# 40 instead of 32 expert products made ahead of the dense loop, 8 of them parked in DRAM

## The chip, the core and the metric

The kernel runs on one core of a Trainium2 chip. The metric is the device time in microseconds (us), the median of several executions. The core has five engines that run their own instruction queues in program order: PE (matmul, with its weight loads PEld), DVE (elementwise), ACT (activations and copies), POOL (here: gathers) and SP (here: most DMA issues). ACT and POOL issue DMAs too.

## The reference, cut to what matters

One decoder block for 512 tokens of width 1024: two token mixers (attention and RWKV-7), then a feed-forward part that picks 128 of 16384 experts for each token. The changed lines belong to that last part:

```
s1, s2 = q1 @ sub_keys1.T, q2 @ sub_keys2.T     # 8 heads, 128 keys each side
expert_idx, gates = top 16 of (top 16 of s1 + top 16 of s2), softmax
u   = expert_down[expert_idx]                   # 128 rows of 1024 for each token
act = gelu(einsum('bpd,bphkd->bphk', h, u))
out = einsum('bphk,bphkd->bpd', gates * act, expert_up[expert_idx])
```

## The kernel before, in words

The 512 tokens are four blocks of 128. For blocks 0 and 1 the chosen expert rows are **gathered**: 256 gathers of 1 MB (`peer`, tiles `gl`), each followed by a dot product and an add on DVE (L1118 and L1124). For blocks 2 and 3 (`DENSE`) every expert is computed: the 16384 experts are 128 groups of 128. For group i, `dense_z(i)` multiplies the down rows (`u_raw`, 512 KB) by the 256 tokens and puts gelu of it into a tile of 128x256, a *product*. The **dense loop** in `dense` then runs rounds 0 to 127: it scales product i by the gates (`G`), loads the up rows (`v_raw`, 512 KB), splits both into a high and a low part (`hi_lo`: a CAST on ACT and a subtraction on DVE), and adds three matmuls for each of four accumulators in PSUM (12 matmuls `acc` a round, of the round before).

Products come in two ways. Those with i < `AZ` = 32 are made **ahead** of the loop from unsplit f32 (`ps_z<-hf,u_raw`; a matmul in the code is two MATMUL records here, 16 a product) and stay in four tiles `A` of eight products. The other 96 are made **in the loop** from split operands (`ps_z<-hh,uh`, `hl,uh`, `hh,ul`: 24 matmuls a product), and for these ACT and DVE also split `u_raw`.

The products ahead are steps of a generator. `ZFIRST` = 12 of them are handed out while the last blocks choose their experts (`tail_c` works through eight heads: queries `ps_q`, scores `ps_sc`, top-16 on DVE; then `select` makes `idx`), two after each step, with a later priority. 16 more come between the 16 steps of `dense_spread`, which turns indices and gates into the gate table `gd` in DRAM: each step writes 1 MB from a tile `g_` (three buffers) with a DMA on ACT's queue. The last 4 are drained at the end of the spreading. The loop's first scaling needs the load `G<-gd`, which needs all 16 writes.

The Tile scheduler orders the instructions of each engine by priority and its own estimate of readiness. The gathers are given a late priority and fill in everywhere, also in the dense loop. All of this is one static order for each engine, so an instruction that waits holds everything behind it on its engine.

Of the kernel before, what the change touches and what calls it, by code (L numbers as in the profile page):

```python
# [9 lines left out]
F32 = mybir.dt.float32  # L10
# [9 lines left out]
P = 128  # L20
# [13 lines left out]
PRE = 2  # L34
LATE = 1000
ZLATE = 100
ZFIRST = 12
AZ = 32
NG = 3
BG = [[0.91, 2, 2, 1.0, 2.2, 2.85, 2.45, 1.0], [1.6, 2.28, 1, 0.58, 0.25, 0.5, 0.13, 0.36]]  # L40
ZSTEP = 2
# [105 lines left out]
def build(tc, A, out):  # L147
    nc = tc.nc
    with ExitStack() as ctx:
        _build(ctx, tc, nc, A, out)  # L150


def _build(ctx, tc, nc, A, out):
# [3 lines left out]
    def pool(name, side="left", space=None, stack=ctx):  # L157
        kw = dict(space=space) if space is not None else dict(side=side)
        return stack.enter_context(tc.tile_pool(name=name, bufs=1, **kw))

    cp = pool("cp")
    dp = pool("dp", space=bass.MemoryType.DRAM)
# [10 lines left out]
    def bank(name, tag, bufs):  # L173
        return pp.tile([P, 512], F32, name=name, tag=tag, bufs=bufs)
# [57 lines left out]
    def mm(o, l, r, start=True, stop=True):  # L232
        PE.matmul(o, l, r, start=start, stop=stop)  # L233
# [722 lines left out]
    def tail_c(blocks, M, tops):  # L956
# [23 lines left out]
        for bb, b in enumerate(blocks):  # L980
            nc.scalar.dma_start(x2d[b * P:(b + 1) * P, :], x2[bb])
            hT2 = (hTr if b in DENSE else Mh)("h2T", [P, KT, P])
            h2T.append(hT2)
            rs = norm(x2[bb], flat(hT2))
            V.tensor_scalar(x2[bb], x2[bb], rs, None, op0=ALU.mult)
            for k4 in range(2):
                ps = psum_x("ps_h2T")
                for j in range(4):
                    k = 4 * k4 + j
                    PE.transpose(ps[:, j * P:(j + 1) * P], x2[bb][:, k * P:(k + 1) * P], ident)  # L990
                for j in range(4):
                    k = 4 * k4 + j
                    S.activation(hT2[:, k], ps[:, j * P:(j + 1) * P], AF.Identity, scale=hA2[:, k:k + 1], bias=hB2[:, k:k + 1])
            if b in DENSE:
                dense_h(b, hT2)
                if b == DENSE[-1]:
                    ahead["z"] = dense_ahead()
            yield
# [140 lines left out]
    SUB = 8  # L1139
    GSC = 2.0 ** 14  # L1140
    nd = len(DENSE) * P
    dn, ahead = {}, {}
    gd = dp.tile([P, P // SUB, nd // TB, SUB * TB], F32, name="gd")

    def hi_lo(hi, lo, x):
        S.copy(hi, x)  # L1146
        V.tensor_tensor(lo, x, hi.bitcast(F32), op=ALU.subtract)  # L1147
# [12 lines left out]
    def dense_z(i):  # L1160

        dz = dn["z"]
        hh_, hl_ = dn["h"]
        if i < AZ:
            if i % SUB == 0:
                dn["A"] = dz.tile([P, SUB, nd], F32, name="A", tag="A", bufs=AZ // SUB)
            act = dn["A"][:, i % SUB]
        else:
            act = dn["v"].tile([P, nd], F32, name="act", tag="act", bufs=2)
        u = dz.tile([P, D], F32, name="u_raw", tag="u", bufs=4)  # L1170
        nc.sync.dma_start(u, A["dense"][i, 0])
        if i < AZ:
            zs = ((u, dn["hf"]),)
        else:
            uh = dz.tile([P, D], F32R, name="uh", tag="uh", bufs=2)
            ul = dz.tile([P, D], F32R, name="ul", tag="ul", bufs=2)
            hi_lo(uh, ul, u)
            zs = ((uh, hh_), (uh, hl_), (ul, hh_))
        ps = bank("ps_z", "pr", 3)
        for k in range(KT):  # L1180
            ks = slice(k * P, (k + 1) * P)
            for m, (l, h) in enumerate(zs):
                mm(ps[:, :nd], l[:, ks], h[:, k], k + m == 0, k == KT - 1 and m == len(zs) - 1)
        S.activation(act, ps[:, :nd], AF.Gelu_apprx_tanh)  # L1184
        dn["act"][i] = act

    def dense_ahead():
        for i in range(AZ):
            dense_z(i)
            yield  # L1190

    def dense_spread(sel):
# [4 lines left out]
        with ExitStack() as own:  # L1197
# [12 lines left out]
            for q, (idx, gates) in enumerate(sel):  # L1210
# [8 lines left out]
                for t0 in range(q * P, (q + 1) * P, TB):  # L1219
                    g_ = dn["g"].tile([P, P // SUB, SUB * TB], F32, name="g_", tag="G", bufs=NG)  # L1220
                    gv = g_.rearrange("p j (c t) -> p (j c) t", t=TB)
# [20 lines left out]
    def dense(sel):  # L1242

        n = nd
        for _ in dense_spread(sel):
            step(ahead["z"])
        drain(ahead["z"])
        dn["v"] = de = pool("de", side="right")
        parts = {}

        def gates_of(j):

            if j < P // SUB:
                parts[j] = dn["g"].tile([P, n // TB, SUB, TB], F32, name="G", tag="G", bufs=NG)
                nc.sync.dma_start(parts[j].rearrange("p s c t -> p s (c t)"), gd[:, j])

        gates_of(0)
        gates_of(1)
        acc = [[bank(f"acc{q}{d}", *(("px", 2) if q == 0 else (("pm", 1), ("po", 1))[d])) for d in range(2)]
               for q in range(len(DENSE))]  # L1260
        prev = None
        for i in range(P + 1):
            if i < P:
                if i % SUB == 0:
                    gates_of(i // SUB + 2)
                if i >= AZ:
                    dense_z(i)
                act = dn["act"].pop(i)
                v = dn["w"].tile([P, D], F32, name="v_raw", tag="v", bufs=4)
                nc.sync.dma_start(v, A["dense"][i, 1])  # L1270
                vh = de.tile([P, D], F32R, name="vh", tag="vh", bufs=2)
                vl = de.tile([P, D], F32R, name="vl", tag="vl", bufs=2)
                hi_lo(vh, vl, v)
                a3 = act.rearrange("p (s t) -> p s t", t=TB)
                V.scalar_tensor_tensor(a3, a3, 1.0 / GSC, parts[i // SUB][:, :, i % SUB], op0=ALU.mult, op1=ALU.mult)
                ch = de.tile([P, n], F32R, name="ch", tag="ch", bufs=2)
                cl = de.tile([P, n], F32R, name="cl", tag="cl", bufs=2)
                hi_lo(ch, cl, act)
                cur = (ch, cl, vh, vl)
            if prev is not None:  # L1280
                ch, cl, vh, vl = prev
                for q in range(len(DENSE)):
                    qs = slice(q * P, (q + 1) * P)
                    for d in range(2):
                        ds = slice(d * 512, (d + 1) * 512)
                        for m, (a, b) in enumerate(((ch, vh), (ch, vl), (cl, vh))):
                            mm(acc[q][d], a[:, qs], b[:, ds], i == 1 and m == 0, i == P and m == 2)
            prev = cur
            yield
        gt2 = dn["z"].tile([P, D], F32, name="gt2", tag="u", bufs=4)  # L1290
        nc.sync.dma_start(gt2, mrow[3:4, :].to_broadcast([P, D]))
        for q, b in enumerate(DENSE):
            x2 = dn["w"].tile([P, D], F32, name="x2e", tag="v", bufs=4)
            y = dn["w"].tile([P, D], F32, name="y", tag="v", bufs=4)
            nc.sync.dma_start(x2, x2d[b * P:(b + 1) * P, :])
            for d in range(2):
                ds = slice(d * 512, (d + 1) * 512)
                V.tensor_tensor(y[:, ds], acc[q][d], gt2[:, ds], op=ALU.mult)
                V.tensor_tensor(y[:, ds], y[:, ds], x2[:, ds], op=ALU.add)
            nc.sync.dma_start(out[b * P:(b + 1) * P, :], y)  # L1300
        yield
# [73 lines left out]
    def step(gen, n=1, ahead=0):  # L1375
        for _ in range(n):
            tc.cur_priority -= ahead
            next(gen, None)
            tc.cur_priority += ahead

    def drain(gen):
        for _ in gen:
            pass
# [30 lines left out]
    for _ in streams[1]:  # L1414
        if "z" in ahead and nz < ZFIRST:
            tc.cur_priority += ZLATE
# [11 lines left out]
    for _ in dense([sel[b] for b in DENSE]):  # L1428
        tc.cur_priority += LATE
        step(gather)  # L1430
        tc.cur_priority -= LATE
# [15 lines left out]
```

## Time and profile before

| | |
|---|---|
| time, median of 3 runs (lowest to highest) | 1959.58 us (1954.78 to 1961.55) |
| the profiled execution: its own time, its span | 1955.61 us, 1953.8 us |
| PE busy | 1719.2 us (88%) |
| DVE busy | 1607.6 us (82%) |
| ACT busy | 708.4 us (36%) |
| DMA, mean | 303 GB/s |
| mean granted TensorE clock | 0.944 of full |

Busy time is a share of the whole span, and the stages differ: up to about 1000 us the mixers, to 1180 us the choice of experts for blocks 2 and 3, to 1295 us the spreading of the gates, from 1320 to 1945 us the dense loop. Matmuls are pipelined, so their own durations overlap; what one costs is read from the distance between two starts. The granted clock has two levels, 1.2 and 2.4 GHz, so 0.50 in a stretch is the lower one throughout.

### The profile page before, as it was taken

The page shows a single profiled execution, that of the slowest core. Times are in us where ns is not written, and L with a number is a line of the kernel's source. Part 1 is how long each engine was busy: PE and PEld are TensorE (multiplying, and loading weights), DVE is VectorE, ACT ScalarE, POOL GpSimd, SP SyncE. Part 2 cuts the span into 40 slices and gives each one's busy share as a digit, 9 for nine tenths or more (in the row PEclk, how much of TensorE's full clock was granted, in tenths as well). Part 3 has the DMA queues.
Part 4 walks back from the last instruction along what each step waited for, and adds up shares of the span by engine and source line. Part 5 has one row for each costly group of instructions (what it writes and reads, how often), then busy time and mean ns, then how long its engine had stood idle before and what let it go on. Part 6 is the DMA issues. An engine that isn't in the chain of part 4 may idle for free.

```text
span 1953.8 us, 30403 instructions
## 1 busy us (share of the span) xinstructions
PE 1719.2 (88%) x11066; PEld 1473.3 (75%) x11066; DVE 1607.6 (82%) x3732; ACT 708.4 (36%) x1733; POOL 475.5 (24%) x394
## 2 busy tenths in 40 slices
PE   2789989999899999994769809969999999999998
PEld 2677777778787788883458807857789998888997
DVE  6675446459778898887789999969999999999995
ACT  1243233421323322231131113334555555555553
POOL 1210010000332200233322243421323233343310
PEclk9899999899899999996879959989999999999999
DMA  7744654066986965888989959998999999999993
GB/s 296 260 151 156 233 179 159 23 223 205 359 347 250 352 232 182 325 303 303 372 329 359 338 198 335 371 359 343 400 389 416 415 416 415 416 414 414 415 370 119
DMA packets 151347, 592.95 MB, mean 303 GB/s; under 512 B 13710, under 2 KB 46734, under 8 KB 116380
## 3 DMA queue, kind: packets, MB, share of 16 engines
q1 hardware_dynamic: 76624, 286.17, 39.3%
q0 software_dynamic: 39360, 280.51, 37.0%
q10 hardware_dynamic: 35212, 24.31, 4.0%
q8 instruction: 87, 1.43, 0.3%
q14 instruction: 64, 0.52, 0.1%
HBM read 568.91 MB, written 22.04 MB: 302 GB/s over the span
## 4 chain that ended last, share of the span: by engine, by line
PE 35%; issue 27%; DMA 15%; DVE 12%; POOL 11%; ACT 0%; POOLq 0%; SPq 0%; DVEq 0%; ACTq 0%
POOL gl L1115 11%; DMA gl<-in_experts,ii 6%; PE ps_b L233 4%; PE acc L233 4%; PE ps_z L233 4%; PE ps_gt L233 3%; DMA w_b<-in_w_b 3%; PE ps_q L233 3%; DVE acc L1124 3%; DVE gl L1118 2%; PE ps_m L233 2%; PE ps_mix L233 2%; PE ps_ap L233 2%; PE ps_M L233 2%; PE ps_y L233 1%
## 5 line engine op out<-in xcount | busy, mean ns | idle before, releaser
L1115 POOL DMA_INDIRECT gl<-in_experts,ii x256 | 420.2, 1641 | 959.5 <-DVE acc L1124 690.7
L1118 DVE SCALAR_TENSOR_TENSOR gl<-gl,h2p 128x1024 f32<-128x1024 f32 x256 | 311.4, 1216 | 42.2 <-DMA gl<-in_experts,ii 41.8
L1124 DVE SCALAR_TENSOR_TENSOR acc<-gl,z,acc 128x1024 f32<-128x1024 f32 x256 | 326.7, 1276 | 2.9 <-ACT z L1120 2.2
L233 PE MATMUL ps_z<-hh,ul 128*128 128x256 f32 x768 | 217.7, 283 | 3.3 <-DVE ul L1147 3.3
L233 PE MATMUL ps_z<-hh,uh 128*128 128x256 f32 x768 | 217.5, 283 | 0.4 <-ACT act L1184 0.4
L233 PE MATMUL ps_z<-hl,uh 128*128 128x256 f32 x768 | 217.6, 283 | 0.0
L233 PE MATMUL acc<-vh,ch 128*128 128x512 f32 x512 | 197.0, 394 | 16.7 <-ACT ch L1146 16.4
L233 PE MATMUL acc<-vh,cl 128*128 128x512 f32 x512 | 202.9, 396 | 3.1 <-DVE cl L1147 3.1
L233 PE MATMUL acc<-vl,ch 128*128 128x512 f32 x512 | 202.5, 396 | 0.7 <-DVE vl L1147 0.7
L1119 ACT ACTIVATE z<-z 128x1 f32<-128x1 f32 x256 | 52.1, 204 | 373.9 <-DVE gl L1118 373.5
L1147 DVE TENSOR_TENSOR vl<-v_raw,vh 128x1024 fp32r<-128x1024 f32 x128 | 156.2, 1220 | 6.8 <-ACT vh L1146 6.6
L233 PEld LDWEIGHTS ps_z<-hh,uh 128*128 128x128 f32 x768 | 146.8, 191 | 4.1 <-ACT act L1184 0.6
L233 PEld LDWEIGHTS ps_z<-hl,uh 128*128 128x128 f32 x768 | 147.1, 192 | 3.6 <-issue 0.2
L233 PEld LDWEIGHTS ps_z<-hh,ul 128*128 128x128 f32 x768 | 147.0, 191 | 3.8 <-DVE ul L1147 3.7
L233 PE MATMUL ps_z<-hf,u_raw 128*128 128x256 f32 x512 | 132.2, 392 | 15.0 <-ACT i1T L1215 15.0
L233 PE MATMUL ps_gt<-hT,w_b 128*128 128x128 f32 x1024 | 136.3, 287 | 9.8 <-DMA w_b<-in_w_b 7.7
L233 PE MATMUL ps_b<-hT,w_b 128*128 128x128 f32 x896 | 127.0, 293 | 14.1 <-DMA w_b<-in_w_b 12.2
L233 PEld LDWEIGHTS ps_gt<-hT,w_b 128*128 128x128 f32 x1024 | 127.2, 200 | 15.7 <-issue 9.6
L1146 ACT CAST vh<-v_raw 128x1024 fp32r<-128x1024 f32 x128 | 134.0, 1048 | 13.2 <-DMA v_raw<-in_dense 8.5
L233 PEld LDWEIGHTS ps_b<-hT,w_b 128*128 128x128 f32 x896 | 116.3, 205 | 24.8 <-issue 10.6
L233 PE MATMUL ps_q<-h2T,w_q 128*128 128x128 f32 x1024 | 127.7, 278 | 1.9 <-DMA w_q<-in_w_query 1.8
L233 PEld LDWEIGHTS ps_q<-h2T,w_q 128*128 128x128 f32 x1024 | 124.3, 194 | 5.1 <-DMA w_q<-in_w_query 2.2
(430 smaller groups left out, 3306.7 us busy)
## 6 DMA issues: line engine op xcount, KB each, us to landing
u_raw<-in_dense SPq DMA_DIRECT2D x128, 512.0 KB
v_raw<-in_dense SPq DMA_DIRECT2D x128, 512.0 KB
w_b<-in_w_b SPq DMA_DIRECT2D x90, 512.0 KB
w_q<-in_w_query SPq DMA_DIRECT2D x48, 512.0 KB
w_ada<-in_w_ada SPq DMA_DIRECT2D x32, 512.0 KB
G<-gd SPq DMA_DIRECT2D x16, 1024.0 KB
w_o<-in_w_o SPq DMA_DIRECT2D x24, 512.0 KB
w_out<-in_w_out SPq DMA_DIRECT2D x24, 512.0 KB
```

The lines of the kernel that those rows point to most:

```text
L233: PE.matmul(o, l, r, start=start, stop=stop)
L1115: G.indirect_dma_start(out=gl, out_offset=None, in_=A["experts"], in_offset=bass.IndirectOffsetOnAxis(ap=ii[:, s:s + 1], axis=0))
L1118: V.scalar_tensor_tensor(gl[:, :D], gl[:, :D], 1.0, h2, op0=ALU.mult, op1=ALU.mult, accum_out=z[:, 0:1])
L1119: S.activation(z[:, 1:2], z[:, 0:1], AF.Gelu_apprx_tanh)
L1124: V.scalar_tensor_tensor(acc, gl[:, D:], z[:, 1:2], acc, op0=ALU.mult, op1=ALU.add)
L1146: S.copy(hi, x)
L1147: V.tensor_tensor(lo, x, hi.bitcast(F32), op=ALU.subtract)
```

## The change

40 products are made ahead instead of 32. `ZFIRST` is 20 instead of 12, so the eight more are handed out before the spreading; 16 still come between its steps and 4 at its end, so these are now products 20 to 39. The four tiles `A` still hold only 32. Products 32 to 39 go through a tile `zp` with two buffers and are written to a DRAM tensor `zd` (128 KB each) by a DMA on ACT's queue. At round 24 a new tile `A` (the buffer of rounds 0 to 7) is loaded with all eight (1 MB, SP's queue). The loop makes 88 products instead of 96.

```diff
-ZFIRST = 12
+ZFIRST = 20
 AZ = 32
+PZ = 8
...
+    zd = dp.tile([P, PZ, nd], F32, name="zd")
...
             act = dn["A"][:, i % SUB]
+        elif i < AZ + PZ:
+            act = dz.tile([P, nd], F32, name="zp", tag="zp", bufs=2)
         else:
...
-        if i < AZ:
+        if i < AZ + PZ:
             zs = ((u, dn["hf"]),)
...
         S.activation(act, ps[:, :nd], AF.Gelu_apprx_tanh)
-        dn["act"][i] = act
+        if AZ <= i < AZ + PZ:
+            nc.scalar.dma_start(zd[:, i - AZ], act)
+        else:
+            dn["act"][i] = act
 
     def dense_ahead():
-        for i in range(AZ):
+        for i in range(AZ + PZ):
...
                     gates_of(i // SUB + 2)
-                if i >= AZ:
+                    if AZ <= i + SUB < AZ + PZ:
+                        t = dn["z"].tile([P, SUB, nd], F32, name="A", tag="A", bufs=AZ // SUB)
+                        nc.sync.dma_start(t, zd[:, i + SUB - AZ:i + 2 * SUB - AZ])
+                        for j in range(SUB):
+                            dn["act"][i + SUB + j] = t[:, j]
+                if i >= AZ + PZ:
                     dense_z(i)
```

What it does to the order is seen in three places. The first is PE, between the queries of the last head (`ps_q`), its scores (`ps_sc`) and the transposes `ps_igT` that open the spreading. Before:

```order
L233 MATMUL ps_q<-h2T,w_q 128x128 x28
L233 MATMUL ps_sc<-sk,qTp 128x128 x4
L1214 MATMUL ps_igT<-cst,idx_8611 128x128 x2
L1214 MATMUL ps_igT<-cst,gates_8582 128x128
L233 MATMUL ps_z<-hf,u_raw 128x256 x6
```

And of the change:

```order
L234 MATMUL ps_q<-h2T,w_q 128x128 x29
L234 MATMUL ps_z<-hf,u_raw 128x256 x2
L234 MATMUL ps_sc<-sk,qTp 128x128 x4
L234 MATMUL ps_z<-hf,u_raw 128x256 x46
L1221 MATMUL ps_igT<-cst,idx_8709 128x128 x2
L1221 MATMUL ps_igT<-cst,gates_8656 128x128
L234 MATMUL ps_z<-hf,u_raw 128x256 x6
```

46 matmuls of products (eight a product in this listing, so nearly six products) now stand behind the last scores; the other two products more stand between the scores of the last two heads. In the spreading itself the pattern of `ps_z` and `ps_G` on PE is nearly that of before.

The second place is ACT, in the spreading steps 10 and 11 of 16 (`ps_G` is copied into `g_`, which is then written to `gd`; `A` or `zp` receives gelu of a product; `z` belongs to the gathers). Before:

```order
L1238 COPY g__9324<-ps_G 128x128x4 x2
L1119 ACTIVATE z<-z 128x1
L1239 DMA gd<-g__9324 2048x1x128
L1238 COPY g__9392<-ps_G 128x128x4 x2
L1184 ACTIVATE A<-ps_z 128x256
L1120 ACTIVATE z<-z,gates_6211 128x1
L1238 COPY g__9392<-ps_G 128x128x4 x2
L1119 ACTIVATE z<-z 128x1
L1239 DMA gd<-g__9392 2048x1x128
```

And of the change:

```order
L1188 ACTIVATE zp<-ps_z 128x256
L1190 DMA zd<-zp 128x256
L1245 COPY g__9422<-ps_G 128x128x4 x2
L1246 DMA gd<-g__9422 2048x1x128
L1245 COPY g__9490<-ps_G 128x128x4 x2
L1188 ACTIVATE zp<-ps_z 128x256
L1120 ACTIVATE z<-z 128x1
L1190 DMA zd<-zp 128x256
L1121 ACTIVATE z<-z,gates_6212 128x1
L1245 COPY g__9490<-ps_G 128x128x4 x2
L1246 DMA gd<-g__9490 2048x1x128
```

The eight `zd` writes alternate with the `gd` writes of steps 10 to 15 on the one queue, and each `zp` from the third on stands ahead of copies of `ps_G`.

The third place is the end of the dense loop on DVE: the last 12 rows ahead of the closing `y<-acc` (`vl` is the low part of `v_raw`, one a round; `ul` that of `u_raw`, one for each product made in the loop; L1132 of the change closes the gathers). Before:

```order
L1275 SCALAR_TENSOR_TENSOR act<-act,G 128x256
L1147 TENSOR_TENSOR cl<-act,ch 128x256
L1147 TENSOR_TENSOR vl<-v_raw,vh 128x1024
L1147 TENSOR_TENSOR ul<-u_raw,uh 128x1024
L1275 SCALAR_TENSOR_TENSOR act<-act,G 128x256
L1147 TENSOR_TENSOR cl<-act,ch 128x256
L1147 TENSOR_TENSOR vl<-v_raw,vh 128x1024
L1275 SCALAR_TENSOR_TENSOR act<-act,G 128x256
L1147 TENSOR_TENSOR cl<-act,ch 128x256
L1147 TENSOR_TENSOR vl<-v_raw,vh 128x1024
L1275 SCALAR_TENSOR_TENSOR act<-act,G 128x256
L1147 TENSOR_TENSOR cl<-act,ch 128x256
```

And of the change:

```order
L1132 TENSOR_TENSOR acc<-acc,e 128x1024
L1149 TENSOR_TENSOR cl<-act,ch 128x256
L1149 TENSOR_TENSOR vl<-v_raw,vh 128x1024
L1149 TENSOR_TENSOR ul<-u_raw,uh 128x1024
L1287 SCALAR_TENSOR_TENSOR act<-act,G 128x256
L1149 TENSOR_TENSOR cl<-act,ch 128x256
L1149 TENSOR_TENSOR vl<-v_raw,vh 128x1024
L1287 SCALAR_TENSOR_TENSOR act<-act,G 128x256
L1149 TENSOR_TENSOR cl<-act,ch 128x256
L1149 TENSOR_TENSOR vl<-v_raw,vh 128x1024
L1287 SCALAR_TENSOR_TENSOR act<-act,G 128x256
L1149 TENSOR_TENSOR cl<-act,ch 128x256
```

The gathers close five rounds nearer to the end: behind the add of the last gather stand nine `vl` and seven `ul` before, and four `vl` and two `ul` in the change. Up to there each round of either version holds about as many gathers. The loads of the spreading and of the loop on SP's queue are in the order of before, with `A<-zd` among the `v_raw` loads of the first rounds; POOL's order is the same.

## Rows read from the trace of the kernel before

**Rows 1.** Windows, one stretch: busy us (instructions) by engine, clock, DMA share

```profile
core 0: us, PE busy (x) PEld busy (x) DVE busy (x) ACT busy (x) POOL busy (x), PEclk, DMA share, GB/s
1123.00:1157.00 34.00, 0.97 (x9) 0.79 (x8) 34.00 (x120) 3.58 (x10) 13.90 (x5) 0.53 0.53 195
```

**Rows 2.** Windows of the dense loop, columns as in rows 1 (PE to POOL)

```profile
1320.00:1420.00 100.00, 98.61 (x413) 78.36 (x414) 95.98 (x147) 54.63 (x101) 23.39 (x13) 0.97 0.95 371
...
1520.00:1620.00 100.00, 100.00 (x644) 91.01 (x643) 99.20 (x132) 55.38 (x112) 35.40 (x20) 1.00 1.02 415
...
1900.00:1954.00 54.00, 46.97 (x294) 42.18 (x293) 30.38 (x42) 20.14 (x31) 0.00 (x0) 0.97 0.39 133
```

**Rows 3.** End of the chain: start us, us, engine and tile

```profile
1933.01 2.87 PE ps_z L233 x24
1938.63 2.87 PE ps_z L233 x24
1941.50 3.44 PE acc L233 x15
```

**Rows 4.** Waits of PE in the dense loop: us in total, times, longest

```profile
PE acc L233 <- ACT ch L1146: 16.4, 2, 16.3
PE acc L233 <- DVE cl L1147: 3.1, 9, 1.0
```

**Rows 5.** Timeline of DVE around the last gather: start us, us, line, operation

```profile
1890.34 1.21 DVE L1118 SCALAR_TENSOR_TENSOR gl<-gl,h2p 128x1024 f32<-128x1024 f32 x1
...
1891.48 1.22 DVE L1147 TENSOR_TENSOR vl<-v_raw,vh 128x1024 fp32r<-128x1024 f32 x1
1892.62 1.27 DVE L1124 SCALAR_TENSOR_TENSOR acc<-gl,z,acc 128x1024 f32<-128x1024 f32 x1
1893.82 0.41 DVE L1275 SCALAR_TENSOR_TENSOR act<-act,G 128x256 f32<-128x256 f32 x1
1894.15 1.21 DVE L1147 TENSOR_TENSOR ul<-u_raw,uh 128x1024 fp32r<-128x1024 f32 x1
...
1895.63 1.27 DVE L1124 SCALAR_TENSOR_TENSOR acc<-gl,z,acc 128x1024 f32<-128x1024 f32 x1
```

**Rows 6.** Timeline of PE, choice of experts; in brackets idle time and releaser

```profile
1063.93 4.91 PE L233 MATMUL ps_z<-hf,u_raw 128*128 128x256 f32 x22
...
1156.92 0.48 PE L1214 MATMUL ps_igT<-cst,idx 128*128 128x128 f32 x1 [33.02 <-DVE idx L1089]
...
1174.54 5.22 PE L233 MATMUL ps_z<-hf,u_raw 128*128 128x256 f32 x12 [15.02 <-ACT i1T L1215]
```

**Rows 7.** Timeline of ACT in the spreading (ACTq: a DMA issue)

```profile
1239.55 0.52 ACTq L1239 DMA_DIRECT2D gd<-g__9256  x1
...
1244.85 0.39 ACT L1184 ACTIVATE A<-ps_z 128x256 f32<-128x256 f32 x1 [1.67 <-PE ps_z L233]
...
1256.12 1.07 ACT L1238 COPY g__9460<-ps_G 128x512 f32<-128x512 f32 x2 [2.59 <-DMA gd<-g__9256]
...
1267.77 5.22 ACTq L1239 DMA_DIRECT2D gd<-g__9528  x1
...
1281.48 0.39 ACT L1184 ACTIVATE A<-ps_z 128x256 f32<-128x256 f32 x1 [1.07 <-PE ps_z L233]
...
1288.21 1.07 ACT L1238 COPY g__9733<-ps_G 128x512 f32<-128x512 f32 x2 [4.95 <-DMA gd<-g__9528]
...
1292.59 0.52 ACTq L1239 DMA_DIRECT2D gd<-g__9733  x1
```

**Rows 8.** Timeline of all engines at the start of the dense loop

```profile
1315.12 1.28 SPq L1255 DMA_DIRECT2D G<-gd  x3
...
1319.81 1.10 DVE L1275 SCALAR_TENSOR_TENSOR A<-A,G 128x256 f32<-128x256 f32 x3 [13.68 <-DMA G<-gd]
...
1320.73 0.80 PE L233 MATMUL acc<-vh,ch 128*128 128x512 f32 x1 [16.26 <-ACT ch L1146]
```

**Rows 9.** DMA queue of ACT, 1160 to 1330 us: packets, MB, share of 16 engines

```profile
q10 hardware_dynamic: 33024, 16.78, 33.0%
```

## Prediction, made before the change was run

> **What bounds the kernel now.** The profile's own execution took 1955.6 us, 4.0 under the median of the runs shown (1959.6); the sum is made against its own time. First I read the chain of what ended last, from its end. There a round of the dense loop starts every 5.62 us (1933.01 to 1938.63), 2.87 us of it the 24 matmuls of a product, so 2.75 us the twelve of `acc`, and the last matmul starts to drain at 1944.9 [rows 3]. Then the windows of the loop: PE, DVE and the DMA are all full at once (100.00 and 99.20 us of 100, 415 GB/s), and only after the last gather, from 1900 us on, is there room: DVE 30.38 us of 54, DMA 133 GB/s [rows 2]. Which of the three is the bound is told by who waits: apart from one wait of 16.3 us at the start, PE lost 3.1 us to DVE in the whole loop [rows 4]. PE's own work sets its length, with DVE close behind.
>
> Next the two places where PE has nothing to do. One lies between the last scores and the spreading: 33.0 us, then 15.0 us more [rows 6], while DVE is busy for all of a window of 34 us that lies in it, the granted clock is 0.53 and the DMA is half used (0.53, 195 GB/s) [rows 1]. The other is the start of the loop: PE starts at 1320.7 after 16.3 us of idling, ACT waited for DVE's first scaling, and that waited for `G<-gd` [rows 8], issued at 1315.1, when the last `gd` write, issued at 1292.6, had landed [rows 7, 8].
>
> **The change part by part.**
>
> *Taken from the loop:* eight products of 2.87 us on PE [rows 3], 23.0 us. DVE loses eight `ul` of 1.14 us (1890.34 to 1891.48 is the distance of such a row to the next [rows 5]), 9.1 us, and the DMA 4.2 MB of `u_raw`.
>
> *Added ahead:* eight products of 16 records. 22 of them took 4.91 us, so about 0.22 us each at the upper clock and 3.5 us a product; after the idle time 12 took 5.22 us, 0.43 us each, 6.9 us a product at the lower clock [rows 6]. Six stand behind the last scores: 21 us, 41 at the lower clock, in 33.0 us of idle time, and the 15.0 us behind it are idle for another reason, so neither delays the transposes that matter. The eight 512 KB loads fall where the DMA is half used; the later ones share SP's queue with `h2p` of the next gather block, and at most wait for a product each. Their gelus, with the exponentials of `select` now between them, need few of ACT's 30 idle us there [rows 1]. If that cover were gone, all eight would cost 28 us. The other two stand ahead of the last scores, which so come up to 7 us later. DVE, which is never idle there, has gathers in its order to do first. Bounds 0 and 7 us; I take 1, since the order gives DVE the same number of gathers before the spreading.
>
> *The writes:* eight of 128 KB on ACT's queue, among sixteen of 1 MB. Those already fall behind: the ninth landed by 1256.1, the thirteenth by 1288.2, the last by 1315.1 (the copy or load that waited for each [rows 7, 8]), four writes in 32.1 us and three in 26.9, 8.0 and 9.0 us for each. ACT's issue itself took 5.22 us once [rows 7]. The loop starts when this queue is empty, so bytes added to it count. Eight writes are the bytes of one `gd` write, at most 9 us; by packets they are 1024 beside 33024 [rows 9], half of a `gd` write, 4 us; if the other queues give way, nothing. I take 5, near the count of packets.
>
> *The wait of `zp`:* two buffers, so from the third product on the gelu waits for the landing of the write two before, and behind it on ACT stand the copies of `ps_G` and the `gd` writes. As long as a `gd` write is on its way during such a wait, the queue that sets the loop's start stays busy, and the wait costs nothing beyond the bytes above. I take 0 and make the upper end a rival.
>
> *The load `A<-zd`:* 1 MB, needed at round 32, 88 us after the loop's start at 2.75 us a round; its buffer is free after round 8. With the `u_raw` loads gone the loop moves 3.1 MB less. 0.
>
> *DVE in the shorter loop:* a gather costs 2.34 us on DVE (1890.34 to 1891.48 and 1892.62 to 1893.82), a round 2.96 (`act` 0.33, `ul` and `cl` 1.48 to the next add, `vl` 1.14 [rows 5]; the same again within 0.01). Up to the last gather DVE now has five more rounds to do, +14.8, eight `ul` less, −9.1, and by the order one gather more after the loop's start, +2.3: the last add, 575.8 us after the start (1319.8 to 1895.6 [rows 5, 8]), comes at 583.8. From there the loop took 49.3 us, 20.1 of it seven products, so 29.2 us or 10.6 rounds for nine `vl`. With four `vl` and two products it takes 5.6 rounds of 2.75 and 5.7 us, 21.1. Together 604.9 against 625.1: 20.2 us less, where PE alone would give 23.0. So DVE keeps 3 of it.
>
> Sum: 1955.6 − 23.0 + 3 (DVE) + 5 (writes) + 1 (scores) = 1941.6. The runs scatter by 7 us and the profiled one is in their lower half; I add half of its 4.0 and say **1943.5**. A difference under 0.3%, about 6 us, can't be told from no change here.
>
> **The rivals.**
>
> *The writes are hidden as well* and DVE finds its time: 1955.6 − 23.0 + 2 = 1934.6. For it: the small writes are one seventeenth of the queue's bytes. Against it: the queue was behind when the last was issued, 22.5 us before it landed [rows 7, 8].
>
> *DVE and the gathers are the bound*, and PE's saving turns into waits: then the loop shrinks by what DVE loses, 9.1 us, less 6 for the later start: 1955.6 − 3 + 2 = 1954.6, too little to be told from no change; half of it would still show (1948). For it: 99.20 us of 100, and 415 GB/s [rows 2]. Against it: the free time after 1900 us, which is where the gathers can spread to.
>
> *Two buffers are too few* (the other side). If a small write takes as long to land as a `gd` write, 16.6 us (1239.55 to 1256.12), 20.4 or 22.5 us [rows 7, 8], the eighth gelu comes three landings after the second: 67.5 us at the longest, where the last eight gelus of before took 36.6 us (1244.85 to 1281.48 [rows 7]). ACT, and with it the copies and `gd` writes, would then be 31 us late: 1955.6 − 20 + 31 + 1 = 1967.6, slower by 0.6%. It decides from a landing of 18.5 us on (3 × 18.5 − 36.6 = 19). Against it: those times include the wait behind two or three earlier 1 MB writes, and an ACT that is held issues none; behind one write it is 8 to 9 us and the rest of a second. The Trainium skill, page "DMA: Bandwidth & Descriptors", section "Queues, rings and completion order", speaks for this rival: each DMA engine takes a queue's descriptors in ring order, so a small write queues behind the `gd` write before it. The trace agrees so far that `gd` writes land one after the other, 8 to 9 us apart [rows 7, 8]. The same page, section "Anatomy of one DMA — SWDGE (gpsimd) path", fits one DMA alone at 2.0 us plus its bytes over 436 GB/s; by that a 128 KB write lands in an estimated 2.3 us, no gelu waits, and the sum would lose its 5 us: 1936.6 on the profile's scale. The 1 MB writes of this case took four to five times what that fit gives them, so I go by the rows.
>
> **How the numbers follow.** Forecast 0.60 (1936 to 1950: the writes from 0 to 9 us, the scores from 0 to 7, DVE from 0 to 5, 2 us of scatter); writes hidden 0.12; DVE and gathers the bound 0.12, half of it showing as faster; two buffers too few 0.16, of which 0.06 only eat the gain and 0.10 make it slower. Faster by over 0.3%: 0.60 + 0.12 + 0.06 = 0.78; within 0.3%: 0.06 + 0.06 = 0.12; slower: 0.10. The range 1931 to 1958 leaves out the slow end of the last rival and a little below the second.
>
> **What would show it.** In the changed profile: the 33 us gap on PE filled by `ps_z<-hf,u_raw`, with the clock at its upper level there; the spreading's first `ps_G` where it was, within some us; ACT's waits for `zd<-zp` few and short; `G<-gd` issued 3 to 9 us later than 1315.1; rounds of 5.62 us at the end of the loop, the last gather's add within some 25 us of the last matmul; and from the loop's start to the last matmul 602 to 606 us. The prediction is wrong if ACT waits for `zd` by tens of us, or if PE waits for `vl` and `cl` by more than some 5 us in the loop.

## The result, and the profile after

The change took 1935.34 us (median of 9 runs, 1924.71 to 1946.50) beside 1958.20 for the kernel before (9 runs): a ratio of 0.991, 95% interval 0.9883 to 0.9938, that is 12 to 23 us faster. The forecast was 1943.5. The profiled execution took 1931.73 us, its span 1930.0.

Before anything else the two traces have to be brought to one starting point. All five engines run the same instructions in the same order up to the queries of the last block, and yet the first transpose of `ps_h2T`, ahead of them, stands 13.3 us earlier in the changed kernel. Timeline of PE, before and after (the idle time ahead of the row in brackets):

```profile
996.40 1.97 PE L990 MATMUL ps_h2T<-cst,x 128*128 128x128 f32 x8 [10.87 <-DVE rsg L272]
```

```profile
983.09 1.97 PE L991 MATMUL ps_h2T<-cst,x 128*128 128x128 f32 x8 [10.88 <-DVE rsg L273]
```

In the profiles of this study that row starts anywhere from 983.1 to 999.9 us, whatever the kernel. So 13.3 of the 23.8 us between the two spans are scatter of the mixers, and the profiles can be compared only from this row on. I cut them there into three stretches by rows of PE: the **choice** of experts (first `ps_h2T` to first `ps_igT` of the spreading), the **spreading** (to the first `acc`), the **loop** (to the end of the last `acc` row; 2.0 us more than the chain's reading in the prediction, in both kernels).

| kernel | choice | spreading | loop | sum | ratio to before (interval) |
|---|---|---|---|---|---|
| before | 160.5 | 163.8 | 626.2 | 950.6 | 1 |
| the change | 166.6 | 163.4 | 610.1 | 940.0 | 0.991 (0.9883 to 0.9938) |
| e1_place | 164.7 | 163.7 | 625.0 | 953.4 | 0.9961 (0.9931 to 0.9991) |
| e2_number | 162.3 | 174.0 | 624.4 | 960.7 | 1.0026 (0.9991 to 1.0061) |
| e3_actout | 163.1 | 170.9 | 610.0 | 944.0 | 0.9941 (0.9914 to 0.9968) |
| e4_sp | 167.1 | 162.1 | 607.2 | 936.3 | 0.9874 (0.9835 to 0.9912) |
| e5_again | | | | | 0.9882 (0.9857 to 0.9907) |
| e6_zp4 | 164.7 | 163.7 | 610.1 | 938.5 | 0.9909 (0.9877 to 0.994) |
| e7_keep5 | 166.6 | 158.9 | 612.1 | 937.6 | 0.9903 (0.9874 to 0.9933) |
| e8_pz16 | 184.8 | 157.6 | 591.5 | 933.8 | 0.9926 (0.9902 to 0.995) |
| e9_park5 | 166.0 | 166.1 | 609.6 | 941.7 | 0.9948 (0.9916 to 0.998) |
| e10_keep5 | 166.7 | 157.1 | 611.4 | 935.2 | 0.9889 (0.984 to 0.9938) |
| e11_sp | 168.1 | 166.2 | 606.0 | 940.3 | 0.9912 (0.988 to 0.9944) |
| e12_keep5_z24 | 167.3 | 158.0 | 608.5 | 933.8 | 0.992 (0.9889 to 0.9952) |

Each stretch is that of one execution. The profile of e5_again fell into a disturbed execution (1958.59 us; its other runs took 1929.36 to 1937.59), so its stretches are left out.

**The choice.** Timeline of PE: the last scores before, and the rows after that answer to [rows 6]:

```profile
1122.73 1.16 PE L233 MATMUL ps_sc<-sk,qTp 128*128 128x128 f32 x8 [2.17 <-ACT qTp L1025]
```

```profile
1116.94 1.13 PE L234 MATMUL ps_sc<-sk,qTp 128*128 128x128 f32 x8
1117.91 20.02 PE L234 MATMUL ps_z<-hf,u_raw 128*128 128x256 f32 x92
1149.69 0.45 PE L1221 MATMUL ps_igT<-cst,idx 128*128 128x128 f32 x1 [11.76 <-DVE idx L1090]
...
1164.82 4.55 PE L234 MATMUL ps_z<-hf,u_raw 128*128 128x256 f32 x12 [12.61 <-ACT i1T L1222]
```

The six products stand in the gap that was empty, 0.22 us a matmul, and 11.76 us of it are left. The windows show the granted clock at its upper level over these products (1.00), where the gap of before had shown 0.53, and the DMA at 325 GB/s (columns as in [rows 1]; from 1150 us on, behind the transposes, the mean is 0.63, so the lower level for much of that stretch):

```profile
1118.00:1138.00 20.00, 19.93 (x93) 17.20 (x91) 20.00 (x83) 6.09 (x14) 4.50 (x4) 1.00 0.89 325
1150.00:1175.00 25.00, 10.86 (x64) 8.63 (x64) 25.00 (x57) 5.70 (x15) 6.74 (x3) 0.63 0.53 186
```

**The spreading.** Timeline of ACT, after, answering to [rows 7]. Small writes now hold ACT in their issue, and the next gelu stands behind it:

```profile
1257.08 8.41 ACTq L1190 DMA_DIRECT2D zd<-zp  x1
...
1265.59 0.38 ACT L1188 ACTIVATE zp<-ps_z 128x256 f32<-128x256 f32 x1 [7.84 <-issue]
...
1277.40 7.25 ACTq L1190 DMA_DIRECT2D zd<-zp  x1
...
1292.62 0.52 ACTq L1246 DMA_DIRECT2D gd<-g__9836  x1
```

The last `gd` write stands at 1292.6 in both traces, but that is not the same place: counted from the first transpose it is issued after 142.9 us (1292.62 − 1149.69), before after 135.7 (1292.59 − 1156.92, [rows 6, 7]). So ACT is 7.3 us later with it.

**The start of the loop.** Timelines of SP, DVE and PE, after, answering to [rows 8]: from the first `ps_h2T` to the issue of `G<-gd` it is 324.0 us (1307.09 − 983.09), 5.3 more than before (1315.12 − 996.40 = 318.7). Those 5.3 lie in the choice: from the first transpose it is 157.4 us, before 158.2. The last `gd` write, issued 7.3 us later, was followed by `G<-gd` after 14.5 us where before it took 22.5.

```profile
1307.09 1.76 SPq L1262 DMA_DIRECT2D G<-gd  x3
...
1312.15 1.09 DVE L1287 SCALAR_TENSOR_TENSOR A<-A,G 128x256 f32<-128x256 f32 x3 [5.14 <-DMA G<-gd]
...
1313.07 0.80 PE L234 MATMUL acc<-vh,ch 128*128 128x512 f32 x1 [9.50 <-ACT ch L1148]
```

**The loop.** PE's waits in it, after (us in total, times, longest), answering to [rows 4]:

```profile
PE acc L234 <- ACT ch L1148: 9.8, 2, 9.5
PE acc L234 <- DVE vl L1149: 4.3, 3, 3.7
PE acc L234 <- DVE cl L1149: 2.4, 7, 0.8
PE acc L234 <- ACT vh L1148: 1.4, 1, 1.4
```

The wait of 3.7 us for `vl` is new. Timelines of SP and DVE show where it comes from: the reload is issued at 1343.52, DVE reaches the first scaling of a reloaded product at 1351.8, in round 14 and not in 32, and stands there for 3.99 us; the `vl` that PE needs is queued behind it.

```profile
1343.52 0.50 SPq L1275 DMA_DIRECT2D A<-zd  x1
...
1351.42 0.42 DVE L1149 TENSOR_TENSOR cl<-A,ch 128x256 fp32r<-128x256 f32 x1
1355.83 0.42 DVE L1287 SCALAR_TENSOR_TENSOR A<-A,G 128x256 f32<-128x256 f32 x1 [3.99 <-DMA A<-zd]
...
1357.18 1.22 DVE L1149 TENSOR_TENSOR vl<-v_raw,vh 128x1024 fp32r<-128x1024 f32 x1
```

At the end a round still takes 5.62 us (the chain, answering to [rows 3]), and the add of the last gather (timeline of DVE, as in [rows 5]) now stands 21 us ahead of the chain's end instead of 49:

```profile
1909.17 2.87 PE ps_z L234 x24
1912.04 2.75 PE acc L234 x12
1914.79 2.87 PE ps_z L234 x24
1917.66 3.45 PE acc L234 x15
```

```profile
1900.06 1.27 DVE L1125 SCALAR_TENSOR_TENSOR acc<-gl,z,acc 128x1024 f32<-128x1024 f32 x1
```

### The profile page after: what moved, and what is told of

The parts are those of the page before. It is cut to its first block, busy times and chain, and to the rows that moved or that the text cites. A ratio compares the mean times of both kernels' runs of the same rounds, so it can differ in the third digit from the quotient of the medians.

```text
span 1930.0 us, 30268 instructions
## 1 busy us (share of the span) xinstructions
PE 1712.6 (89%) x11002; PEld 1465.1 (76%) x11002; DVE 1597.4 (83%) x3724; ACT 702.8 (36%) x1727; POOL 447.9 (23%) x394
## 4 chain that ended last, share of the span: by engine, by line
issue 31%; PE 28%; DMA 14%; POOL 13%; DVE 12%; ACT 1%; POOLq 0%; SPq 0%; DVEq 0%; ACTq 0%
POOL gl L1116 13%; DMA gl<-in_experts,ii 6%; PE ps_b L234 4%; PE ps_q L234 3%; DMA w_b<-in_w_b 3%; PE ps_gt L234 3%; DVE acc L1125 2%; DVE gl L1119 2%; DMA w_out<-in_w_out 2%; PE ps_m L234 2%; PE ps_ap L234 2%; PE ps_mix L234 2%; DMA w_ada<-in_w_ada 2%; PE ps_y L234 1%; PE ps_s L234 1%
## 5 line engine op out<-in xcount | busy, mean ns | idle before, releaser
L1116 POOL DMA_INDIRECT gl<-in_experts,ii x256 | 393.6, 1537 | 988.5 <-DVE acc L1125 727.1
L234 PE MATMUL ps_z<-hh,ul 128*128 128x256 f32 x704 | 199.5, 283 | 2.4 <-DVE ul L1149 2.4
L234 PE MATMUL ps_z<-hh,uh 128*128 128x256 f32 x704 | 199.4, 283 | 0.4 <-ACT act L1188 0.4
L234 PE MATMUL ps_z<-hl,uh 128*128 128x256 f32 x704 | 199.6, 283 | 0.0
L234 PE MATMUL ps_z<-hf,u_raw 128*128 128x256 f32 x640 | 160.2, 391 | 12.6 <-ACT i1T L1222 12.6
L234 PEld LDWEIGHTS ps_z<-hf,u_raw 128*128 128x128 f32 x640 | 116.9, 195 | 31.6 <-ACT i1T L1222 13.0
L1148 ACT CAST vh<-v_raw 128x1024 fp32r<-128x1024 f32 x128 | 134.1, 1048 | 16.2 <-DMA v_raw<-in_dense 10.1
L234 PEld LDWEIGHTS ps_z<-hh,uh 128*128 128x128 f32 x704 | 134.6, 191 | 7.0 <-issue 3.1
L234 PEld LDWEIGHTS ps_gt<-hT,w_b 128*128 128x128 f32 x1024 | 126.0, 199 | 16.2 <-issue 11.1
L234 PEld LDWEIGHTS ps_z<-hl,uh 128*128 128x128 f32 x704 | 134.8, 192 | 3.1
L234 PEld LDWEIGHTS ps_z<-hh,ul 128*128 128x128 f32 x704 | 134.7, 191 | 2.7 <-DVE ul L1149 2.6
```

The lines of the kernel that those rows point to most:

```text
L1116: G.indirect_dma_start(out=gl, out_offset=None, in_=A["experts"], in_offset=bass.IndirectOffsetOnAxis(ap=ii[:, s:s + 1], axis=0))
```

## The experiments

My theory after the result: the gain is the loop's shorter PE work, 23.0 us, less small prices ahead of it (the later scores, the writes) and less the stand at the reload. The main rival: the gain comes from filling PE's empty time ahead of the spreading. Twelve runs were made: nine other kernels, two of them twice, and the change once more.

**e1_place and e2_number: the two halves of the change alone.**

```diff
-PZ = 8            # e1: 20 ahead of the spreading, 32 in all
+PZ = 0
...
-ZFIRST = 20       # e2: 40 in all, 12 ahead of the spreading
+ZFIRST = 12
```

> Placement alone: 20 products ahead of the spreading as in the change, but 32 products in all, none in DRAM, 96 made in the loop. Three stretches are compared, by rows of PE: choice (first ps_h2T to first ps_igT: 160.5 us before, 166.6 in the change), spreading (to the first acc: 163.8 and 163.4), loop (to the end of the last acc: 624.2 and 608.0). Theory (the gain is the loop's shorter work, less small costs ahead of it): choice 164 to 168, spreading 150 to 164, loop 622 to 626; time within 10 us of before. Rival (the gain comes from filling PE's empty time ahead of the spreading, so the clock is higher behind it): choice and spreading together 10 us or more shorter than before, and the time at least 10 us below before.

> Number alone: 40 products, eight of them through DRAM as in the change, but only 12 ahead of the spreading, so 28 come in it and at its end. Theory: choice as before (160 to 161 us), loop as in the change (606 to 610), spreading longer than before by what of eight products (28 us at the upper clock) the wait for the last gd write does not cover, 5 to 22 us; time from 12 us below before to 8 above. Rival (placement is the gain): no gain left, and 15 us or more slower than the change.

e1: choice 164.7, spreading 163.7, loop 625.0; ratio 0.9961, 1950.38 us beside 1953.57. Choice and spreading together are 4.1 us longer than before, where the rival had them 10 us shorter, and the loop is that of before. In time the interval leaves a gain of 2 to 13 us, so a part of the change's gain in time is not excluded here; its trace from the first `ps_h2T` on, 2.8 us longer than before, shows none.

e2: spreading 174.0, 10.2 longer than before, as the theory has it; but the loop took 624.4 and not 606 to 610. The reason is in the order: before and in the change, five products of the loop stand ahead of its first `acc` on PE (4.7 in the change), where PE waits for `G` anyway; in e2 none does, because the products at the end of the spreading have taken that place, so its loop contains 4.7 more than the change's, 13.5 us by 2.87 each (610.1 and 13.5 are 623.6). The gain is gone (ratio 1.0026). Both halves are needed: eight products fewer in the loop pay only if the eight have an empty place ahead of it.

**e3_actout: the reloaded products scaled into another tile.**

```diff
+                if AZ <= i < AZ + PZ:
+                    act = de.tile([P, n], F32, name="act", tag="act", bufs=2)
+                s3 = act.rearrange("p (s t) -> p s t", t=TB)
-                V.scalar_tensor_tensor(a3, a3, ...)
+                V.scalar_tensor_tensor(s3, a3, ...)
```

> The change, with the scaling of the eight reloaded products into a tile of two buffers instead of in place, so that DVE reaches it some rounds later. Theory: in the change DVE stood 4.0 us at the first such scaling, waiting for the reload, and PE 3.8 us for the low part queued behind it; here that wait is 0 to 1 us and the loop 603 to 606 us instead of 608.0, other stretches unchanged. Rival (the loop there is held by the loads of v_raw, which come late anyway): the wait goes to v_raw and the loop stays at 607 to 609.

Nothing waits for `zd` any more, and DVE's 4.0 us are gone. But the loop took 610.0 us. Two things took the gain. The loads of `v_raw` come late in that part as well (the waits of its first 150 us):

```profile
ACT vh L1148 <- DMA v_raw<-in_dense: 12.4, 8, 3.7
...
PE acc L234 <- ACT vh L1148: 2.3, 1, 2.3
PE acc L234 <- DVE vl L1149: 1.3, 3, 0.5
PE acc L234 <- DVE cl L1149: 0.4, 1, 0.4
```

which is 4.0 us of PE's waits beside 5.7 for `vl` and `vh` in the change. And the scaled products hold the two `act` buffers, so by the order only three products of the loop stand ahead of its first `acc` instead of 4.7: 4.9 us more inside it (41 matmuls of 0.12). So theory and rival were each half right on the wait, and this kernel's time says nothing on it. Its spreading took 170.9 us, 7.5 more than the change's, with that part in the change's order or nearly so: one execution can differ by that much.

**e4_sp and e11_sp: the eight writes on SP's queue.**

```diff
-            nc.scalar.dma_start(zd[:, i - AZ], act)
+            nc.sync.dma_start(zd[:, i - AZ], act)
```

> The change, with the eight writes of parked products issued by SP instead of ACT. In the change four of these issues held ACT for 4.15, 4.14, 8.41 and 7.25 us, and yet the last gd write was issued at the same distance from the transposes as before. Theory: those stalls only take the place of waits that the gd writes would have had, and spreading gets shorter by 0 to 3 us (161 to 164). Rival (ACT's stalls are the price of the writes): spreading shorter by 10 us or more. A second rival (the two buffers): a write on SP's queue lands later, ACT waits for zp, and spreading gets longer by 5 us or more.

> e4_sp once more with more rounds: by the theory that the writes cost the gd queue their bytes and ACT its stalls, time 2 to 6 us below the change (ratio to before 0.986 to 0.990); if moving them changes nothing, 0.990 to 0.993.

Spreading took 162.1 and 166.2 us, with the writes on ACT 163.4 (the change) and 163.7 (e6). On SP an issue takes 0.33 to 1.24 us. In e11 (the rows that touch `zd`: ns min/median/max):

```profile
L1190 SPq DMA_DIRECT2D zd<-zp x8: 326/422/1242, 1246.9 to 1290.1; - x8
L1275 SPq DMA_DIRECT2D A<-zd x1: 424/424/424, 1351.8 to 1351.8; - x1
```

ACT is held all the same, now in its 1 MB issues. Its timeline in e4:

```profile
1257.95 6.34 ACTq L1246 DMA_DIRECT2D gd<-g__9490  x1
...
1289.76 5.19 ACTq L1246 DMA_DIRECT2D gd<-g__9766  x1
```

The issues of `gd` and `zd` that held ACT for over 1 us add up to 30.4 us in e4 and 17.3 in e11, to 29.3 in the change (24.0 of them in small writes) and 19.9 before. So the stalls pass to the `gd` writes, as the theory has it (its "same distance" for the last `gd` write is a misreading: 142.9 us and 135.7, see above). The spreading does not follow them: in e11 ACT was held 12 us less than in the change, and the spreading is 2.8 longer. Both rivals of e4 are out by their own bounds, but a spreading without such stalls was not tried. The times, 0.9874 and 0.9912, lie on both sides of the change, and cannot be told from it.

In both runs nobody waited for the reload, and the loops, 607.2 and 606.0, are 3 to 4 us shorter than the change's. DVE came for it no later: 8.4 us after its issue, in the change 8.3. So the load landed sooner. The DMA queues in these 8.3 us, in the change and below it in e11 (packets, MB, share of 16 engines; q0 carries the gathers, q1 SP's loads):

```profile
q0 software_dynamic: 234, 1.65, 50.7%
q1 hardware_dynamic: 364, 1.67, 49.8%
```

```profile
q1 hardware_dynamic: 371, 1.89, 59.9%
q0 software_dynamic: 138, 1.05, 30.3%
```

The late landing goes with more of the gathers beside the load. e4 (1.05 MB) and e6 (1.61 MB, with the wait) fit this; no run changed the gathers alone.

**e5_again and e6_zp4: the change once more, and with four `zp` buffers.**

```diff
-            act = dz.tile([P, nd], F32, name="zp", tag="zp", bufs=2)
+            act = dz.tile([P, nd], F32, name="zp", tag="zp", bufs=4)
```

> The change once more, as it is: how much of its stretches is its own and how much one execution. Theory: choice 163 to 168 us, spreading 161 to 171, loop 607 to 611; the wait of DVE for the reload anywhere from 0 to 4 us, since e4_sp with the same place of the scaling did not show it. Rival (the 4.0 us wait for the reload is fixed by the order): it comes again, 3 to 5 us.

> The change with four zp buffers instead of two. Theory: what held ACT in the change were the issues of the writes on its own queue, not a zp buffer that a landing had to free; spreading stays at 161 to 171 us, and ACT's issues of zd writes still take 4 to 8 us three or four times. Rival (two buffers are too few): spreading 5 us or more shorter than e5_again of this call, and the stalls gone.

e5 repeats the change's time (ratio 0.9882). In e6 no `zp` waits for a landing any more, and still the issues stall ACT and the spreading takes 163.7 us. Rows of `zp` in e6, and below them what ended ACT's idle time ahead of them:

```profile
L1190 ACTq DMA_DIRECT2D zd<-zp x8: 327/2626/7076, 1242.9 to 1291.1; - x8
...
  issue: 6.5, 1
```

So in the change the two buffers were not what held ACT. The reload was waited for again: DVE 3.9 us, PE 3.5 us for `vl`, with the loop at 610.1 as in the change.

**e7_keep5, e9_park5, e10_keep5: the trip through DRAM by itself.** e7 and e10 are one kernel: 37 products ahead, the five beyond the tiles `A` in five `zp` tiles that are used where they lie. e9 sends the same five through DRAM.

```diff
-PZ = 8
+PZ = 5
...
-            act = dz.tile([P, nd], F32, name="zp", tag="zp", bufs=2)     # e7, e10
+            act = dz.tile([P, nd], F32, name="zp", tag="zp", bufs=PZ)
...
-                        nc.sync.dma_start(t, zd[:, ...])                  # e9
+                        nc.sync.dma_start(t[:, :PZ], zd)
```

> 37 products ahead, five beyond the four tiles kept in SBUF, nothing written to DRAM and nothing reloaded; 91 products in the loop. Theory (the DRAM trip costs 0 to 3 us, a product in the loop 2.87): loop 612 to 616 us, spreading 158 to 170 as in the change, time 4 to 9 us above the change. Rival (the trip through DRAM eats a good part of the gain): as fast as the change or faster, though three more products are made in the loop.

> 37 products ahead as in e7_keep5, but the five beyond the tiles go through DRAM as in the change (two zp buffers, five writes, one reload of 640 KB). Against e10_keep5 of this call it has the trip and nothing else. Theory after the runs so far (the trip costs about 4 us in the spreading and about 4 at the reload, eight in all for eight products): spreading 3 to 6 us longer than e10_keep5, loop 2 to 5 longer, time 3 to 9 us longer. Rival (the trip is free, and e7_keep5's shorter spreading was one execution): both stretches within 2 us, time within 3.

> e7_keep5 once more, beside e9_park5: spreading 156 to 163 us, loop 610 to 614, time 15 to 21 us below before by the theory that the trip is not free; if it was one execution, spreading 161 to 170 and time 10 to 14 below before.

e7 (0.9903) cannot be told from the change (0.991), though three more products, 8.6 us, stand in its loop. Its loop and its spreading lie in the theory's bounds, and its ratio lies between those of the change (e5) and of e6 measured beside it, 0.9882 and 0.9909. So neither theory nor rival is settled by it, and e9 was made to size the trip. Timeline of PE, the first transpose and the first `acc`, in e9 (with the trip) and in e10 (without):

```profile
1160.81 0.45 PE L1221 MATMUL ps_igT<-cst,idx 128*128 128x128 f32 x1 [13.22 <-DVE idx L1090]
...
1326.89 0.79 PE L234 MATMUL acc<-vh,ch 128*128 128x512 f32 x1 [12.36 <-ACT ch L1148]
```

```profile
1166.46 0.45 PE L1217 MATMUL ps_igT<-cst,idx 128*128 128x128 f32 x1 [8.95 <-DVE idx L1090]
...
1323.61 0.79 PE L234 MATMUL acc<-vh,ch 128*128 128x512 f32 x1 [8.95 <-ACT ch L1147]
```

166.1 against 157.1 us, 9.0 longer (7.2 against e7). In e9 one small write held ACT for 9.21 us, and a little later, from 1288.0 to 1293.7 us, nothing moved on ACT's queue. ACT's timeline, and the only queue with packets in that window:

```profile
1271.71 9.21 ACTq L1190 DMA_DIRECT2D zd<-zp  x1
```

```profile
q0 software_dynamic: 119, 0.97, 55.8%
```

So there ACT's hold, and not only the bytes, may be what the trip costs; but e10's queue has empty stretches too, and without any small write the spreading took from 157.1 (e10) to 163.8 us (before; e1 163.7). One execution of each does not size the price. The loop was 1.8 shorter with the trip, against the theory: in e9 the reload was issued 25.1 us after the first `acc` and landed in time, so nothing waited for it. The times, 0.9948 and 0.9889, differ by 0.6%, with intervals that overlap a little.

**e8_pz16: 48 products ahead, 28 of them ahead of the spreading.**

```diff
-ZFIRST = 20
+ZFIRST = 28
-PZ = 8
+PZ = 16
```

> 48 products ahead, 16 of them through DRAM, 28 ahead of the spreading; 80 in the loop. By the order nearly 13 products now stand behind the last scores, where the change had nearly six and 11.8 us of PE left empty. Theory: the seven more are 24.5 us, so the transposes come about 13 us later (choice 174 to 182 us), the loop is 15 to 22 us shorter than in the change (588 to 595), less than 23 because the last gather's add now closes the loop; time 10 us below the change to 4 above. Rival (there is room for more): choice no more than 3 us longer than in the change, time 15 us or more below the change.

The loop took 591.5 us, another 18.6 less, and the spreading 157.6. But PE had no gap left behind the last scores (its timeline there):

```profile
1126.82 27.28 PE L234 MATMUL ps_z<-hf,u_raw 128*128 128x256 f32 x124
1155.10 3.69 PE L234 MATMUL ps_z<-hf,u_raw 128*128 128x256 f32 x16 [1.00 <-DMA u_raw<-in_dense]
1161.25 16.11 PE L234 MATMUL ps_z<-hf,u_raw 128*128 128x256 f32 x66 [2.46 <-DMA u_raw<-in_dense]
1177.20 0.53 PE L1221 MATMUL ps_igT<-cst,idx 128*128 128x128 f32 x2
```

The transposes stood behind them, and the choice took 184.8 us, 18.2 more than in the change and more than the 174 to 182 expected. The two cancel; 0.9926 is the change's time again. The rival (room for more) is out. And the loop gave 18.6 of 23.0: the chain that ended last runs over the gathers and DVE's sums there, up to the end of the loop, where in the change its end is PE's rounds:

```profile
1918.27 1.20 DVE acc L1125
...
1920.52 1.27 DVE acc L1125
```

So with sixteen products less DVE and the gathers close the loop.

**e12_keep5_z24: four more of e7's products ahead of the spreading.**

```diff
-ZFIRST = 20
+ZFIRST = 24
```

> e7_keep5 with 24 of its 37 products ahead of the spreading instead of 20. Theory (what is left empty on PE behind the last scores, 12.7 us, takes 3.6 products more, and the spreading is set by the gd writes, not by PE): choice 0 to 4 us longer than e10_keep5, spreading 0 to 3 shorter, time within 4 us of e10_keep5. Rival (PE sets the spreading, 97% busy as it is there): spreading 8 to 14 us shorter, time 6 us or more below e10_keep5.

Choice 167.3 (0.6 more than e10), spreading 158.0 (0.9 more): the gap took them for nothing, and the spreading gave nothing back, so PE does not set it, as far as one execution of each shows. Time 0.992, not to be told from e10. None of these kernels is clearly faster than the change; e4_sp and e7_keep5 are its equals.

## Why the prediction was right, point by point

Its sum was −14.0 us on the profile's scale. From the first `ps_h2T` on, the two profiles differ by −10.5, the times by −12 to −23. The loop is 16.2 us shorter where the sum had 20.2; the difference is the stand at the reload. Ahead of the loop the sum had 6 us more, and 5.7 came, but not where it put them: 6.1 in the choice and −0.4 in the spreading. That this total agrees is partly luck. The measured 1935.3 lies next to the rival "writes are hidden" (1934.6), but does not speak for it: that rival has 21 us, and the comparable part of the traces 10.5. What the one profile of before does not hold of the −17.6 (0.991 × 1958.2) I can't place; the kernels with the change's loop and eight writes lie between 936.3 and 944.0 in that stretch, before at 950.6.

- **Taken from the loop, 23.0.** Right. Eight products less, and the round is 5.62 us as before; from DVE's first scaling, as the prediction counts, to the last matmul it took 609.0 us, with 604.9 in the sum and 602 to 606 named as the sign; the rest is the stand at the reload, below. e8 takes eight more out and gets 18.6, for there DVE closes the loop.
- **The scores, 1 us.** Within its bounds, but small. The scores came 7.5 us later (126.3 us from the first `ps_h2T` before, 133.9 after), the two products of 3.5 ahead of them; the transposes still 6.1, but the 15.0 us behind those shrank to 12.6, so the first product of the spreading is 3.6 us late. e1 shows 1.7 of that.
- **The writes, 5 us (0 to 9).** Not sized. Of the change alone they show nothing from the first transpose to the issue of `G<-gd` (157.4 us, before 158.2) and 2.1 from the first product to the first `acc` (146.2 to 148.3). In e9 against e10 and e7 the spreading is 9.0 and 7.2 us longer with five writes, but stretches of one execution scatter by as much (e3, with that part in the change's order or nearly so, has 155.8 from the first product). In time the whole trip, reload included, costs about three products, 8.6 us: with the eight writes the ratios are 0.9874 to 0.9912, without them and with three products more in the loop 0.9903 and 0.9889, each good to some 6 us. Whether the queue's bytes are the price, as the prediction put it, or ACT's holds, stays open: e4 and e11, with the same bytes on the other queue, cannot be told from the change, and in e9 ACT's queue stood empty after a hold.
- **The wait of `zp`, 0, and the rival "two buffers are too few".** The rival is out, by e6. ACT was held, for 24 us, but in the issue of its own writes. The sequence that I gave for it (ACT late, so `gd` writes late) did follow, by 7.3 us from the first transpose (142.9, before 135.7), and cost nothing: the queue was less behind, and `G<-gd` followed 14.5 us after the last write's issue and not 22.5. The Trainium skill, page "Perfetto Trace Analysis", section "DMA Instruction — HWDGE (DVE, Sync)", has an issue last until all its descriptors are generated, with a buffer that can be full; the trace agrees so far that one and the same issue of 128 KB lasts 0.33 us at the least and 8.41 at the most. Whether a full buffer made the long ones no run here shows.
- **The load `A<-zd`, "needed at round 32 … 0".** This is the step that failed, and its size is 4.0 us. The program needs it at round 32, but the order puts the first scaling of a reloaded product on DVE behind 14 `vl`, in round 14: 38.8 us after the first `acc` and not 88, and only 8.3 us after the load's issue. It landed 12.3 us after its issue. e6 shows the same 3.9. In e4 and e11 DVE came as soon, but the load had landed, with 1.05 MB of gathers beside it instead of 1.65 (e6 1.61): the order makes the wait possible, and whether it came went with that traffic, which no run changed by itself.
- **DVE, 3 us.** Right to some tenths but for that stand. From the first scaling to the last gather's add it took 587.9 us (1312.15 to 1900.06; forecast 583.8, and DVE stood 4.0 of the difference), from there to the chain's end 21.0 (forecast 21.1). The sign that I named for being wrong (PE waiting over some 5 us for `vl` and `cl`) did appear, 6.7 us, but 3.7 of it is the reload.
- **The rival "DVE and the gathers are the bound"** is out for the change: its loop fell by 16.2, with sixteen products less (e8) by 34.8. But there PE's waits for `vl` and `cl` are 9.8 us in all and the chain's end is DVE's, so it is the next bound.

## What to carry to other kernels

Work moved out of a full loop pays by what it leaves there, but only up to the empty place that takes it: six products filled 20 of the 33 us and delayed nothing behind them, seven more cost as much as they saved. When a tile is reloaded, look up in the order where its first reader stands on its engine, not at which iteration the program needs the value. And before two profiles are compared, find the first instruction that the change moves, and count from it: here over half of the difference lay ahead of it, and two writes that both stand at 1292.6 us were 7.3 us apart, counted from the transposes.

## What the runs showed of the hardware that was not expected

A write of 128 KB, issued on ACT's queue between writes of 1 MB, held ACT for 0.33 to 8.41 us in its issue (9.21 in e9), on SP's queue for no more than 1.24. The 1 MB issues take 0.52 us where they are not held, and were held as well: for 5.22 us at the most before, 6.34 in e4, 8.79 in e1, which has no small writes. So a long issue is not a matter of the write's size alone. A load of 1 MB landed 12.3 us after its issue with 1.65 MB of gathers moved in its first 8.3 us, and within 8.4 with 1.05. And ahead of any moved instruction the kernels reached the same row between 983.1 and 999.9 us, in a program on one core.
